# One slot 480 bytes longer: where weight tiles and activation slots begin in a partition

## The chip, the core and the metric

The program runs on one core of a Trainium2 chip. What counts is the device time of one execution in microseconds (us). In the profile PE is TensorE's matmul side, PEld its weight loads, DVE VectorE, ACT ScalarE, POOL GpSimd and SP the engine that issues the transfers.

## What is computed

Two transformer blocks, one after the other, on 512 tokens of width 1024, all in float32. Cut to its products, the reference is:

```python
def first_block(x, mem, ...):
    proj = rmsnorm(x) @ w_in                    # 1024 -> 1536: pool mixer, gating unit
    h = x + concat([pool_mixer(p), sgu_mixer(u, v)]) @ w_out
    h = h + mem_cross_attention(rmsnorm(h), mem, wq, wk, wv, wo)   # 4 heads, 256 memory rows
    h = h + conv_ffn(rmsnorm(h), w_up, conv_w, conv_b, w_down)     # 1024 -> 2*2816 -> 1024
    return rmsnorm(h)

def second_block(x, ...):
    q, k, v, glu_a, glu_b = split(rms_norm(x) @ w_in)
    attn = stick_breaking_attention(rms_norm(q), rms_norm(k), v)   # 8 heads
    c = silu(layer_norm(causal_depthwise_conv(glu_a * sigmoid(glu_b))))   # 31 taps
    x = x + concat([attn, c]) @ w_out
    gate, val = split(rms_norm(x) @ w_up)
    return x + (silu(causal_depthwise_conv(gate)) * val) @ w_down
```

## The kernel before

**Products.** Each float32 operand is held as two tiles, a rounded high part (h) and the rest (l), and each product is three matmuls (`mm3`, lines 122 to 125): high by high, high by low, low by high. The first operand of `pe.matmul` after the output is the stationary one, loaded 128x128 ahead of the matmul; the second streams past it (the moving one, mostly 512 columns). Every matmul of `mm3` has a stationary block of its own to load.

**Weights.** A unit is 128x2048 floats. `prep` (lines 174 to 205) transfers it into `raw`, ScalarE casts it into `whi` (line 195) and VectorE subtracts for `wlo` (line 196); `weights` keeps two units ready. `raw`, `whi` and `wlo` have two buffers each. In `sta_unit` (line 212) 128x128 blocks of `whi` and `wlo` are stationary and the activations move: 48 matmuls for a unit with 8 steps of k, in the order whi, whi, wlo. In `mov_stage` (line 222), `project` and `values` the weights move and activations are stationary. Three early units of the second block (`split_early`, line 676) are not in `whi` and `wlo` but in the slots F, G and E.

**Slots.** Activations live in slots of 128x2048 floats, named A0 to H1 (`slot`, line 145); a name is used again and again, as a tile of its own each time. H0 and H1 are longer: `slot("H0", F32R, 2176)` and `slot("H1", F32R, 2056)` at line 403, the same sizes again at lines 637, 905 and 992.

**Where tiles begin.** Each partition is filled in the order constants, slots in the order in which their names first occur, weight tiles, temporary tiles. In the built program the slots come as A0, A1, B0, B1, C0, C1, D0, G0, E0, E1, F0, F1, G1, H0, H1, D1. A slot is 8192 bytes in a partition (16 times 512), H0 8704 (17 times 512), H1 8224 (16 times 512 and 32). A0 begins 96 bytes beyond a multiple of 512 and so do all slots up to H1; D1, which lies behind H1, and then raw, whi, wlo and t2 begin 128 beyond one. A step of k, of a unit's block or of 128 tokens is a multiple of 512 bytes, so that every block of a tile begins at its tile's remainder. The trace names a tile by its letter alone: D stands for D0 and D1.

**The order around the change.** The program order on each engine is set by a scheduler when the kernel is built. In the first block's feed-forward (`evac1`, lines 648 to 657), each unit's result goes from PSUM into H (line 651, after a small memset at line 650), through three taps (lines 643 to 646), a Silu (line 656) and a product (line 657); `work` (line 639) hands out the two halves of H0 and H1 in turn. `col(16)` (line 113) gives small tiles with 8 buffers: four are asked for in the pool mixer (line 390), four in the two calls of `heads` (line 730).

Of the kernel before, what the change touches and what calls it, by code (L numbers as in the profile page):

```python
# [10 lines left out]
F32 = mybir.dt.float32  # L11
F32R = mybir.dt.float32r
# [4 lines left out]
P = 128  # L17
# [3 lines left out]
KC = D // P  # L21
M = 256
# [53 lines left out]
def block_kernel(  # L76
# [17 lines left out]
    tp = ctx.enter_context(tc.tile_pool(name="tp", bufs=4))  # L94
# [16 lines left out]
        return tp.tile([P, 512], F32, tag="t2", name="t2", bufs=2)  # L111

    def col(n):
        return tp.tile([P, n], F32, tag=f"col{n}", name=f"col{n}", bufs=8)

    def keep(name, n=4):
        return const.tile([P, n], F32, tag=name, name=name)
# [27 lines left out]
    def slot(name, dt=F32R, cols=2048):  # L145
        return slots.tile([P, cols], dt, tag=name, name=name)

    def part(tl, a, b, at=0):
        return tl[:, at : at + a * b].rearrange("p (a b) -> p a b", a=a)
# [161 lines left out]
    def mean_col(tiles, w, n=D):  # L311
        nt = w // P
        ps = single()
        chunks = [tl[:, j, :] for tl in tiles for j in range(tl.shape[1])]
        for t in range(nt):
            for i, ch in enumerate(chunks):
                pe.matmul(ps[:, t : t + 1], ch[:, t * P : (t + 1) * P], ones[:, 0:1],  # L317
                          start=i == 0, stop=i == len(chunks) - 1)
        m = col(4)
        dve.tensor_scalar(m[:, :nt], ps[:, :nt], 1.0 / n, EPS, ALU.mult, ALU.add)  # L320
        return m

    def rsqrt(m, n, name=None):
        o = keep(name) if name else col(4)
        pool.tensor_tensor(o[:, :n], m[:, :n], mhalf[:, :n], ALU.pow)
        return o
# [37 lines left out]
    for u in range(2):  # L364
# [23 lines left out]
        for j in range(2):  # L388
            g = 2 * u + j
            hd = col(16)  # L390
            dve.tensor_tensor(hd, sums[j][:, 0:16], par("inv", 16 * g, 16), ALU.mult)
            dve.scalar_tensor_tensor(sums[j], sums[j], 0.5 ** (g + 1), p[:, j, :],
                                     ALU.mult, ALU.subtract)
            dve.tensor_tensor(sums[j][:, 0:16], hd, p[:, j, 0:16], ALU.subtract)
            copy_split(dh[:, g, :], dl[:, g, :], sums[j])
# [4 lines left out]
    gr = slot("G1")  # L400
    sgh, sgl, plh, pll = (part(gr, 4, P, 512 * i) for i in range(4))
    memst = Stats(M)
    mh, ml = part(slot("H0", F32R, 2176), KC, M), part(slot("H1", F32R, 2056), KC, M)

    pool.affine_select(out=sgw, in_=sgw, compare_op=ALU.is_ge, fill=0.0, base=0,
                       pattern=[[0, 4], [1, P]], channel_multiplier=-1)
# [227 lines left out]
        down(2)  # L634

    turn = [0]
    ht = [slot("H0", F32, 2176), slot("H1", F32, 2056)]

    def work(n):
        turn[0] = (turn[0] + 1) % 4  # L640
# [462 lines left out]
```

## Time and profile before

| | us |
|---|---|
| median of three runs | 1275.32 |
| lowest, highest | 1274.69, 1275.57 |
| the profiled execution | 1275.78 |
| its span, first to last instruction | 1274.1 |
| TensorE's granted clock, mean | 0.996 of full speed |
| PE busy | 1257.1 (99%) |
| PEld busy | 1011.6 (79%) |
| DVE busy | 772.2 (61%) |
| ACT busy | 485.1 (38%) |

Matmuls overlap in the pipeline: a 128x512 matmul is shown as about 396 ns long, but the next one starts well before it ends. What a matmul costs in a stream is the distance from its start to the next one's start, called the pitch below. It is read from the timeline, whose start times have two decimals, over many matmuls.

### The profile page before, as it was taken

How to read it: one execution, taken by the hardware profiler on the slowest of the kernel's cores; microseconds unless marked ns; L12 is line 12 of the kernel's file. 1: busy time of each engine (PE TensorE's matmuls, PEld its weight loads, DVE VectorE, ACT ScalarE, POOL GpSimd, SP SyncE). 2: the span in 40 equal slices, each digit the busy share in tenths (PEclk: the TensorE clock that was granted, in tenths of full speed). 3: DMA queues.
4: the chain of work that ended last, by engine and by line, in shares of the span. 5: the costliest groups of instructions: out<-in, count | busy, mean ns of one | idle time of the engine just before them, and what ended most of it. 6: DMA issues, size and time to landing. Idle time of an engine off the chain costs nothing.

```text
span 1274.1 us, 13633 instructions
## 1 busy us (share of the span) xinstructions
PE 1257.1 (99%) x5712; PEld 1011.6 (79%) x5712; DVE 772.2 (61%) x813; ACT 485.1 (38%) x528; POOL 108.7 (9%) x125
## 2 busy tenths in 40 slices
PE   9999999999999999999999899999999999999998
PEld 6888888788888888888887678667888888888887
DVE  7845624744866664466366999976675555336522
ACT  6432524532544432243253225873443333213310
POOL 1100210012000000000054411000400000000000
PEclk9999999999999999999999989999999999999999
DMA  7233222312222222222343001101222222222212
GB/s 285 91 112 109 99 99 74 126 66 100 94 77 95 99 99 99 100 82 85 116 149 132 0 34 67 67 1 66 99 100 99 76 90 99 100 100 100 87 63 81
DMA packets 20445, 118.32 MB, mean 93 GB/s; under 512 B 2208, under 2 KB 4128, under 8 KB 7712
## 3 DMA queue, kind: packets, MB, share of 16 engines
q1 hardware_dynamic: 20096, 117.20, 26.1%
q8 instruction: 44, 0.72, 0.2%
q10 hardware_dynamic: 288, 0.26, 0.1%
q14 instruction: 17, 0.14, 0.0%
HBM read 115.35 MB, written 2.10 MB: 92 GB/s over the span
## 4 chain that ended last, share of the span: by engine, by line
PE 92%; DVE 4%; ACT 2%; issue 1%; POOL 1%; DMA 0%; SPq 0%; DVEq 0%; ACTq 0%
PE pp L124 28%; PE pp L125 28%; PE pp L123 28%; DVE H L832 2%; PE ps L123 1%; PE ps L124 1%; PE ps L125 1%; POOL col L739 0%; DVE H L698 0%; PE ps L317 0%; PE ps L813 0%; DVE t L785 0%; PE pp L774 0%; DMA A<-in_xT 0%; ACT t L783 0%
## 5 line engine op out<-in xcount | busy, mean ns | idle before, releaser
L195 ACT CAST whi<-raw 128x2048 fp32r<-128x2048 f32 (+3 forms) x109 | 197.8, 1815 | 452.4 <-PE pp L124 381.9
L196 DVE TENSOR_TENSOR wlo<-raw,whi 128x2048 fp32r<-128x2048 f32 (+3 forms) x109 | 236.8, 2173 | 73.2 <-ACT whi L195 72.6
L123 PE MATMUL pp<-B,whi 128*128 128x512 f32 x672 | 265.8, 397 | 1.0 <-ACT whi L195 1.0
L125 PE MATMUL pp<-B,wlo 128*128 128x512 f32 x672 | 266.3, 396 | 0.2
L124 PE MATMUL pp<-C,whi 128*128 128x512 f32 x672 | 266.0, 396 | 0.0
L124 PE MATMUL pp<-G,whi 128*128 128x512 f32 x448 | 177.8, 397 | 0.0
L125 PE MATMUL pp<-F,wlo 128*128 128x512 f32 x416 | 164.9, 396 | 0.0
L123 PE MATMUL pp<-F,whi 128*128 128x512 f32 x416 | 164.2, 396 | 0.0
L123 PEld LDWEIGHTS pp<-B,whi 128*128 128x128 f32 x672 | 126.3, 188 | 32.1 <-ACT whi L195 1.8
L125 PEld LDWEIGHTS pp<-B,wlo 128*128 128x128 f32 x672 | 126.2, 188 | 32.1 <-DVE wlo L196 1.5
L124 PEld LDWEIGHTS pp<-C,whi 128*128 128x128 f32 x672 | 126.3, 188 | 30.7 <-issue 0.5
L124 PEld LDWEIGHTS pp<-G,whi 128*128 128x128 f32 x448 | 84.2, 188 | 20.4 <-issue 0.2
L625 DVE TENSOR_TENSOR A<-pp,A 128x1024 f32<-128x1024 f32 x23 | 28.2, 1225 | 112.2 <-PE pp L125 112.2
L125 PEld LDWEIGHTS pp<-F,wlo 128*128 128x128 f32 x416 | 78.2, 188 | 19.0 <-issue 0.2
L646 DVE SCALAR_TENSOR_TENSOR H<-H,sm,H 128x512 f32<-128x512 f32 x132 | 92.8, 747 | 0.7
L123 PEld LDWEIGHTS pp<-F,whi 128*128 128x128 f32 x416 | 78.1, 188 | 19.0 <-issue 0.2
L832 DVE SCALAR_TENSOR_TENSOR H<-H,sm,H 128x512 f32<-128x512 f32 x120 | 88.3, 765 | 1.2
L651 DVE TENSOR_TENSOR H<-pp,rb 128x1024 f32<-128x1024 f32 x22 | 26.9, 1224 | 56.2 <-PE pp L125 49.8
L128 ACT ACTIVATE H<-H,sm 128x512 f32<-128x512 f32 x70 | 54.2, 808 | 9.8 <-DVE H L698 9.8
L997 DVE TENSOR_TENSOR H<-pp,rb 128x512 f32<-128x512 f32 x22 | 15.2, 692 | 67.7 <-PE pp L125 61.3
L124 PE MATMUL pp<-E,whi 128*128 128x512 f32 x112 | 44.3, 396 | 0.0
L123 PE MATMUL pp<-D,whi 128*128 128x512 f32 x112 | 44.2, 395 | 0.0
(293 smaller groups left out, 1808.8 us busy)
## 6 DMA issues: line engine op xcount, KB each, us to landing
raw<-in_wts SPq DMA_DIRECT2D x99, 1024.0 KB, 4.8
raw<-in_wts SPq DMA_DIRECT2D x8, 768.0 KB, 4.2
A<-in_xT SPq DMA_DIRECT2D x3, 512.0 KB, 6.8
out<-A SPq DMA_DIRECT2D x3, 512.0 KB, 2.8
D<-in_memT SPq DMA_DIRECT2D x1, 1024.0 KB, 11.6
raw<-in_wts SPq DMA_DIRECT2D x3, 256.0 KB, 7.1
A<-in_xT SPq DMA_DIRECT2D x2, 256.0 KB, 3.4
raw<-in_wts SPq DMA_DIRECT2D x2, 128.0 KB, 3.6
```

Source lines behind the costliest of these rows:

```text
L123: pe.matmul(out, wh, xh, start=start, stop=False, **kw)
L124: pe.matmul(out, wh, xl, start=False, stop=False, **kw)
L125: pe.matmul(out, wl, xh, start=False, stop=stop, **kw)
L128: act.activation(out, in_, AF.Identity, scale=scale, bias=bias)
L195: act.copy(hi[:, cs], raw[:, cs])
L196: dve.tensor_tensor(lo[:, cs], raw[:, cs], hi[:, cs].bitcast(F32), ALU.subtract)
L625: dve.tensor_tensor(hu, pt, hu, ALU.add)
L646: dve.scalar_tensor_tensor(dst, hs[:, k : k + 512], w(k), dst, ALU.mult, ALU.add)
L651: dve.tensor_tensor(hs[:, :, 2:], pt, over2(rb), ALU.mult)
L832: tap = dve.scalar_tensor_tensor(cv[:, i, :], cc[:, i, k : k + 512], par("dw_w", 4 * k + i), cv[:, i, :], ALU.mult, ALU.add)
L997: dve.tensor_tensor(hs[:, 2:514], pt[:, 0, :], rb, ALU.mult)
```

## The change

H1 gets 2176 columns as H0 has, which is 480 bytes more in each partition (8704 bytes, 17 times 512). All that lies behind it moves by 480: D1, raw, whi, wlo and t2 now begin 96 bytes beyond a multiple of 512, as the slots before H1 do. The three buffers of t4, 128, 256 and 384 before, begin at 96, 224 and 352, the two of acc at 480 instead of 0. The 16-wide small tile has 6 buffers instead of 8, 128 bytes less.

```diff
     def col(n):
-        return tp.tile([P, n], F32, tag=f"col{n}", name=f"col{n}", bufs=8)
+        return tp.tile([P, n], F32, tag=f"col{n}", name=f"col{n}", bufs=6 if n == 16 else 8)
...
-    mh, ml = part(slot("H0", F32R, 2176), KC, M), part(slot("H1", F32R, 2056), KC, M)
+    mh, ml = part(slot("H0", F32R, 2176), KC, M), part(slot("H1", F32R, 2176), KC, M)
...
-    ht = [slot("H0", F32, 2176), slot("H1", F32, 2056)]
+    ht = [slot("H0", F32, 2176), slot("H1", F32, 2176)]
```

No engine gets an instruction more or less, and none changes its place. What differs is a few waits around H1 in `evac1`. On GpSimd, in the first block's feed-forward (H_2137 is H0, H_2138 is H1; lines with a minus are of the kernel before):

```order
 L650 MEMSET H_2137 128x2x2 [waits DVE_49,Activation_49]
-L650 MEMSET H_2138 128x2x2 [waits DVE_49]
+L650 MEMSET H_2138 128x2x2 [waits DVE_49,Activation_49]
 L650 MEMSET H_2137 128x2x2 [waits DVE_49,Activation_49]
-L650 MEMSET H_2138 128x2x2 [waits DVE_49,Pool_49]
+L650 MEMSET H_2138 128x2x2 [waits DVE_49,Activation_49]
```

The memset of H1 waits for ScalarE as well, as that of H0 does; on VectorE the instruction of line 651 that writes H1 then waits for GpSimd, which before stood at the first tap behind it (line 646).

## Rows read from the trace of the kernel before

**Rows 1.** The page: busy time by engine (with its share of the span and the number of instructions), then the chain that ended last, by engine and by line.
```profile
PE 1257.1 (99%) x5712; PEld 1011.6 (79%) x5712; DVE 772.2 (61%) x813; ACT 485.1 (38%) x528; POOL 108.7 (9%) x125
PE 92%; DVE 4%; ACT 2%; issue 1%; POOL 1%; DMA 0%; SPq 0%; DVEq 0%; ACTq 0%
```

**Rows 2.** Busy time in a stretch of 100 us. Columns: the stretch, its length, then busy us with the number of instructions for PE, PEld, DVE, ACT and POOL, the granted clock, DMA's share and GB/s.
```profile
400.00:500.00 100.00, 100.00 (x430) 80.54 (x430) 63.37 (x66) 37.84 (x42) 0.82 (x8) 1.00 0.27 95
```

**Rows 3.** Timeline of PE in the first block's feed-forward, 520 to 534 us: start, shown length, line, output<-moving,stationary tile. The rows shown are the first two and the last of 62 matmuls that follow on each other.
```profile
519.66 0.40 PE L124 MATMUL pp<-E,whi 128*128 128x512 f32 x1
519.89 0.39 PE L125 MATMUL pp<-D,wlo 128*128 128x512 f32 x1
...
533.88 0.40 PE L125 MATMUL pp<-F,wlo 128*128 128x512 f32 x1
```

**Rows 4.** Timeline of PE in the second block, 690 to 694 us and 699.8 to 713.3 us: the end of a weight unit from whi and wlo, then `mov_stage` with the early units of slots F and G moving and slots B and C stationary. Between the rows of 691.24 and 693.30 8 matmuls are left out; from 699.83 to 713.20 there are 60 matmuls with these two ends.
```profile
690.77 0.40 PE L124 MATMUL pp<-C,whi 128*128 128x512 f32 x1
691.01 0.40 PE L125 MATMUL pp<-B,wlo 128*128 128x512 f32 x1
691.24 0.39 PE L123 MATMUL pp<-F,B 128*128 128x512 f32 x1
...
693.30 0.39 PE L123 MATMUL pp<-F,B 128*128 128x512 f32 x1
...
699.83 0.39 PE L123 MATMUL pp<-G,B 128*128 128x512 f32 x1
...
713.20 0.39 PE L125 MATMUL pp<-G,C 128*128 128x512 f32 x1
```

**Rows 5.** Timeline of PE in the first block's `mov_stage`, 34 to 38 us, where whi and wlo move and slots B and C are stationary: the first row and the last of 18 matmuls that follow on each other.
```profile
33.61 0.40 PE L125 MATMUL pp<-whi,C 128*128 128x512 f32 x1
...
37.58 0.40 PE L124 MATMUL pp<-wlo,B 128*128 128x512 f32 x1
```

**Rows 6.** Weight loads on PEld by tiles, first in 520 to 534 us, then in 698 to 713 us: busy us, mean ns of one, idle time before them.
```profile
L123 PEld LDWEIGHTS pp<-F,whi 128*128 128x128 f32 x19 | 3.6, 188 | 0.9
L123 PEld LDWEIGHTS pp<-G,B 128*128 128x128 f32 x14 | 2.6, 188 | 0.5
```

**Rows 7.** Timeline of PE in the pool mixer's product (slots E moving, G1 stationary), 78.6 to 82 us: the second and the last of its 12 matmuls and the one behind them.
```profile
79.06 0.39 PE L124 MATMUL pp<-E,G 128*128 128x512 f32 x1
...
81.37 0.40 PE L125 MATMUL pp<-E,G 128*128 128x512 f32 x1
81.61 0.28 PE L123 MATMUL pp<-H,whi 128*128 128x256 f32 x1
```

**Rows 8.** Timeline of PE in the cross-attention's product of probabilities and values, 246.8 to 252 us: slots F and G move, D0 (lines 123 and 124) and D1 (line 125) are stationary. From 246.88 to 251.08 there are 18 matmuls.
```profile
246.88 0.40 PE L123 MATMUL pp<-F,D 128*128 128x512 f32 x1
247.11 0.40 PE L124 MATMUL pp<-G,D 128*128 128x512 f32 x1
247.35 0.39 PE L125 MATMUL pp<-F,D 128*128 128x512 f32 x1
...
251.08 0.39 PE L123 MATMUL pp<-B,whi 128*128 128x512 f32 x1
```

**Rows 9.** Timeline of PE where 256 columns move: slots E against B and C in the scores, 36 matmuls from 200.59 to 204.90, then H against whi and wlo, 10 matmuls from 94.75 to 95.93.
```profile
200.59 0.28 PE L123 MATMUL pp<-E,B 128*128 128x256 f32 x1
...
204.90 0.40 PE L123 MATMUL ps<-whi,H 128*128 128x512 f32 x1
...
94.75 0.28 PE L123 MATMUL pp<-H,whi 128*128 128x256 f32 x1
...
95.93 0.28 PE L124 MATMUL pp<-H,whi 128*128 128x256 f32 x1
```

**Rows 10.** Instructions that read or write whi, then those of wlo, by stretches: length, busy us with count for PE, PEld, DVE and (whi) ACT, clock, DMA.
```profile
0.00:690.00 690.00, 576.97 (x1885) 349.52 (x1886) 142.72 (x67) 119.27 (x67) 1.00 0.31 109
690.00:870.00 180.00, 67.79 (x212) 39.30 (x212) 14.64 (x7) 13.36 (x7) 0.97 0.10 36
870.00:1274.00 404.00, 357.93 (x1137) 213.26 (x1136) 79.46 (x36) 65.12 (x35) 1.00 0.26 91
0.00:690.00 690.00, 366.20 (x942) 176.99 (x942) 142.72 (x67) 1.00 0.31 109
690.00:870.00 180.00, 42.20 (x107) 19.90 (x106) 14.64 (x7) 0.97 0.10 36
870.00:1274.00 404.00, 224.92 (x569) 106.72 (x568) 79.46 (x36) 1.00 0.26 91
```

**Rows 11.** Busy time by stretches in the middle of the second block, columns as in rows 2.
```profile
690.00:735.00 45.00, 39.76 (x171) 31.71 (x169) 39.87 (x42) 12.22 (x12) 18.91 (x12) 0.93 0.07 25
735.00:760.00 25.00, 25.00 (x102) 20.21 (x101) 22.69 (x30) 4.06 (x5) 0.00 (x0) 0.92 0.12 43
800.00:840.00 40.00, 36.02 (x247) 25.24 (x246) 39.11 (x48) 36.80 (x46) 0.00 (x0) 1.00 0.14 52
```

**Rows 12.** Timeline of POOL, ACT and DVE around a unit of the first feed-forward, 338 to 354 us: the memset, the Silu and the reading of PSUM into H.
```profile
338.89 0.10 POOL L650 MEMSET H<- 128x4 f32 x1 [9.20 <-DVE H L646]
338.14 0.63 ACT L656 ACTIVATE H<-H 128x512 f32<-128x512 f32 x1 [3.06 <-DVE H L646]
342.62 1.23 DVE L651 TENSOR_TENSOR H<-pp,rb 128x1024 f32<-128x1024 f32 x1 [1.67 <-PE pp L125]
```

## The prediction

> **What bounds the kernel now.** I read the page's first part and the chain of waits first. PE is busy for 1257.1 of 1274.1 us, and the chain that ended last is 92% PE and 4% DVE [rows 1]. So nearly everything is one stream of matmuls, and the question is what one matmul costs in it. A stretch of 100 us in the feed-forward holds 430 matmuls with PE never idle and the clock at its full share [rows 2]. The timeline gives the pitch more closely: from 519.66 to 533.88 us there are 61 steps, 14.22 / 61 = 0.2331 us [rows 3]. At the granted full clock of 2.4 GHz 512 columns would be 512 / 2.4 = 213.3 ns, so about 20 ns of each matmul are something else, in a stream without waits. Whether the change can take some of that away is the whole case, because it adds and removes no instruction.
>
> The trace holds the experiment already. At 691.24 us PE goes over from a unit of whi and wlo to `mov_stage` with early units in slots. There both the moving tiles (F, G) and the stationary ones (B, C) are slots that begin 96 bytes beyond a multiple of 512, while nearly everywhere else one of the two is whi or wlo, at 128. The shape, the three matmuls of a product and a new stationary block for each are the same. From 699.83 to 713.20 us there are 59 steps: 13.37 / 59 = 0.2266 us [rows 4]. That is 6.5 ns less than 233.1, through 60 matmuls in a row. The same function in the first block, with whi and wlo moving at 128 and slots B and C stationary at 96, has 17 steps in 3.97 us, 0.2335 [rows 5]: one function, one order of the three products, and what differs for PE is where its tiles begin. The engines beside PE do not explain it: VectorE is busy for 39.87 of 45 us around that stretch [rows 11], and 63.37 of 100 in the feed-forward [rows 2]; PE is faster beside the busier one.
>
> The lower pitch is not there at once. From 691.24 to 693.30, at the entry, 9 steps take 2.06 us, 0.229 each [rows 4]. The pool mixer's 12 matmuls, where E and G1 are both at 96, are over before they are past such an entry: 11 steps from 79.06 to 81.61 us, 0.232 [rows 7]. I take that as one thing: a stream in which all tiles have one remainder settles to 226.6 after some eight matmuls, and an odd tile keeps it from settling. Where D1, at 128, is the stationary tile of one matmul in three, 18 matmuls take 4.20 us, 0.2333, though the other two have equal remainders [rows 8]. So equality in most matmuls buys nothing; all have to be equal, and this is what the move of D1 and of all weight tiles by 480 bytes gives.
>
> **The change part by part.**
>
> *Matmuls with 512 columns and a tile of whi or wlo.* Up to 690 us 1885 and 942 matmuls touch whi and wlo [rows 10], of which 192 move only 256 columns (k of the cross-attention: 4 units of 16 blocks, three matmuls each): 1885 + 942 - 192 = 2635. From 870 us on it is 1137 + 569 = 1706, of which 32 have acc as the moving tile (half of the convolution's part of the output projection), which goes from 0 to 480 and stays odd: 1674. Together 4309. All the other tiles of these streams (B to G, H0, and now D1 and t2) will begin at 96. If each settles, the gain is 4309 x (233.1 - 226.6) = 4309 x 6.5 ns = 28.0 us, all of it on the path, since PE never idles in these stretches.
>
> *The middle, 690 to 870 us.* 212 + 107 = 319 such matmuls lie here [rows 10]. They would give at most 2.1 us, but VectorE is busy for 39.87 of 45 us, 22.69 of 25 and 39.11 of 40 [rows 11]; it carries the 31-tap convolution, and PE waits for it. I take 0.5 us, with 0 and 2.1 as ends.
>
> *The product with D1.* 48 matmuls at 233.3 ns [rows 8] would settle too: 48 x 6.7 = 0.3 us gained.
>
> *Matmuls with 256 columns.* Equal remainders are worse here: in the scores 36 steps take 4.31 us, 0.1197, while H against whi and wlo takes 1.18 us for 10, 0.118 [rows 9]. 192 matmuls go from the second kind to the first: 192 x 1.7 ns = 0.3 us lost.
>
> *Entries.* Each time the stream is broken by another tile or a wait (the sums of the norms against constant tiles, the transposes, the values between the scores), it has to settle again. An entry costs 9 matmuls at 229 instead of 226.6, 0.02 us [rows 4]; an odd tile in between may cost as much as 8 x 6.5 ns = 0.05. With some 30 such places I take 1.0 us; the ends are 0.5 and 3.
>
> *Waits around H1.* The memset of H1 on GpSimd now waits for ScalarE, and the reading of PSUM into H1 on VectorE waits for the memset. Behind it on VectorE stand the split of the next weights and the taps; PE would wait for them last. The tile H0 has these waits already, and the trace shows what they cost: the Silu ends at 338.14 + 0.63 = 338.77, the memset runs at 338.89 for 0.10 us, and the next reading of PSUM begins at 342.62, for PE's sake [rows 12]. The unit that comes next is 48 x 6.5 ns = 0.3 us earlier after the change, against a slack of 3.6 us. So this is nothing; without that cover it would be 0.1 us in each of 11 units, 1.1 us in all.
>
> *Fewer small tiles.* With 6 buffers instead of 8 the last requests in `heads` take buffers that the pool mixer used and left hundreds of us before. Nothing.
>
> *ScalarE, VectorE and the transfers.* raw, whi and wlo have one remainder before and after, so no row prices their moves; I leave casts and subtractions as they are. Should they get 0.1 us longer or shorter they would still be hidden: a unit has 48 x 0.2266 = 10.9 us, and VectorE is busy for 63% of the time in the feed-forward stretch shown [rows 2].
>
> The sum: 28.0 + 0.5 + 0.3 - 0.3 - 1.0 = 27.5 us gained. The profiled execution took 1275.78 us, its span 1274.1, with 1.7 us around it that do not change. 1275.78 - 27.5 = 1248.3; the median of the three runs is 0.5 below the profiled one, so 1275.32 - 27.5 = 1247.8. I say 1248.
>
> **A rule against the change.** The weight loads are shown with 188 ns in the slow stream and in the quick one [rows 6]. So the load's own time does not tell the two apart, and the pitch does. The Trainium skill, "TensorE: Matmul & The Clock Gate", Part 2, Step-by-step, says that PE has two independent SBUF read ports, so that loading the next stationary block takes no bandwidth from the running matmul. By that rule where the two tiles begin would change nothing, and the time would stay at 1275.3. The trace does not agree in so far as the pitch depends on the pair of tiles: 233.1 [rows 3] and 226.6 [rows 4].
>
> **The rivals.**
>
> 1. *The quick stretch is quick for another reason, and nothing changes* (1275.3). For it: in it the weights move, while in most of the kernel they are stationary, and no stretch of the trace has weights at rest in a stream of equal remainders. Against it: the weights move in the first block's `mov_stage` too, and there the pitch is 0.2335 [rows 5]. 6%.
>
> 2. *The stream settles only in part.* If other work breaks it up again and again, it stays in the entry's mean of 0.229 to 0.232 [rows 4, 7]: 4309 x (233.1 - 231.8) = 5.6 us up to 4309 x (233.1 - 229) = 17.7 us gained, 1258 to 1270. For it: the pool mixer never settled. Against it: 60 matmuls in a row did without one odd step, with VectorE at work all the time. 10%.
>
> 3. *Slower: the loss of the 256-column streams is what equal remainders do, and it comes to the 512-column ones with the weights at rest.* There a settled stream of equal remainders has 1.7 ns more for each matmul [rows 9]. Paid in 4309 matmuls it is 7.3 us, 1282.6. It decides from the first 200 matmuls of the first units on. For it: it is a settled stream, of 36 matmuls, and its stationary tiles change every second or third matmul as in `sta_unit`. Against it: with 512 columns the only settled stream went the other way, by four times as much. 4%.
>
> **How the numbers follow.** The forecast, settling nearly everywhere, has 80%: 1248, with its own ends at 1275.3 - (28.0 + 2.1 + 0.3 - 0.5) + 0.3 = 1245.7 and, with entries at 3 us, the waits at 1.1 and nothing from the middle, 1275.3 - (28.0 + 0.3 - 0.3 - 3 - 1.1) = 1251.4. A pitch read from two decimals is good to 0.2 ns, 1 us either way. So 1244.5 to 1252.5 for the forecast alone; a stream that is unsettled for a fifth of its matmuls would add 5.6 us to 1248, and to hold the time in 8 of 10 cases I let the range reach over most of that: 1244 to 1256. What a measurement of this kernel can tell from no change is about 0.2%, 2.6 us. Faster by more than that are the forecast and rival 2, 80 + 10 = 90%; within it is rival 1 with 6%; slower is rival 3 with 4%.
>
> **What would show it right or wrong.** In the profile of the changed kernel a stretch of 100 us in the feed-forward should hold 441 matmuls instead of 430, and the timeline there should have a pitch of 0.2266 with a shown length near 0.39 instead of 0.40. The scores should stay at 0.12, k of the cross-attention go from 0.118 to 0.12, the product with D1 from 0.2333 to 0.2266. VectorE's chain between 690 and 735 us should take as long as before. A pitch that stays at 0.233 where all tiles begin at 96 would make the prediction wrong at its root; one that goes to and fro between 0.225 and 0.236 means rival 2; and a PE that begins to wait for wlo or H in the feed-forward would show a cover that I counted on gone.

## The result, and the profile after

| | before | after |
|---|---|---|
| median, us | 1275.44 | 1246.88 |
| lowest, highest, us | 1274.69, 1276.63 | 1246.36, 1247.21 |
| the profiled execution, us | 1275.78 | 1246.8 |
| its span, us | 1274.1 | 1245.1 |

The kernel after takes 0.9775 of the time before, with a 95% interval of 0.9758 to 0.9792, from four runs of each. It is faster by 28.56 us between the medians, 29.0 between the profiled executions; the forecast had 27.5.

The page of the kernel after, busy time by engine and the chain that ended last by engine:

```profile
PE 1226.2 (98%) x5712; PEld 1009.9 (81%) x5712; DVE 771.2 (62%) x813; ACT 485.2 (39%) x528; POOL 110.0 (9%) x125
...
PE 92%; DVE 4%; ACT 2%; issue 1%; POOL 1%; DMA 0%; SPq 0%; DVEq 0%; ACTq 0%
```

Against [rows 1] one number has moved: PE has 30.9 us less, with the same 5712 matmuls. The other engines work as long as before, and the chain has the same shares: no new wait has taken the place of the gain, the same stream has become shorter.

Busy time in a stretch of the kernel after, columns as in [rows 2]:

```profile
400.00:500.00 100.00, 100.00 (x443) 82.81 (x442) 60.06 (x61) 36.09 (x38) 0.71 (x7) 1.00 0.27 95
```

443 matmuls where 430 stood, at the same granted clock of 1.00, again without an idle moment. The timeline of PE in the kernel after, first block's feed-forward, names the pitch; the three rows are the first two and the last of 63 matmuls that follow on each other:

```profile
519.82 0.39 PE L124 MATMUL pp<-G,whi 128*128 128x512 f32 x1
520.05 0.39 PE L125 MATMUL pp<-F,wlo 128*128 128x512 f32 x1
...
533.87 0.39 PE L123 MATMUL pp<-F,whi 128*128 128x512 f32 x1
```

62 steps in 14.05 us are 0.2266 us, where [rows 3] gave 0.2331. The cross-attention's product with D0 and D1, in the kernel after:

```profile
243.03 0.39 PE L123 MATMUL pp<-F,D 128*128 128x512 f32 x1
...
247.79 0.39 PE L123 MATMUL pp<-B,whi 128*128 128x512 f32 x1
```

21 steps in 4.76 us are 0.2267, against 0.2333 in [rows 8]. And k of the cross-attention, 256 columns, in the kernel after:

```profile
86.98 0.28 PE L124 MATMUL pp<-H,whi 128*128 128x256 f32 x1
...
88.78 0.28 PE L124 MATMUL pp<-H,whi 128*128 128x256 f32 x1
```

15 steps in 1.80 us are 0.120, against 0.118 in [rows 9]: the one kind of stream that became slower, as foretold.

**Where the 29.0 us came from.** The 5712 matmuls stand in the same order with the same operands in both traces, so each step from one start to the next can be set beside its counterpart. Up to the first matmul of the early units (691.24 us before, [rows 4]; 675.79 after) 15.45 us are gained, from there to line 895 (863.61 before, 845.46 after) 2.70, and from there to the end 10.82. By kind of step, worked out from all steps of the two profiled executions, where a 512-column step between 200 and 250 ns counts as one without a wait:

| us gained | forecast | measured |
|---|---|---|
| 512-column steps without a wait, up to the early units | 17.1 + 0.3, less entries | 16.99 |
| the same, from the early units to line 895 | 0.5 | 1.70 |
| the same, from line 895 on | 10.9, less entries | 10.87 |
| entries, all stretches | -1.0 | in the rows above |
| 256 columns | -0.3 | -0.33 |
| waits and other matmuls, up to the early units | 0 | -1.22 |
| the same, in the middle | 0 | 1.01 |
| the same, at the end | 0 | -0.05 |
| sum | 27.5 | 28.97 |

Two lines, -1.22 and 1.01, nobody had foretold. The first comes from one wait at the start. PE in the kernel before, then in the kernel after, at the seventh matmul of the first unit:

```profile
8.25 0.50 PE L123 MATMUL pp<-B,whi 128*128 128x512 f32 x1 [0.16 <-ACT whi L195]
```
```profile
9.33 0.50 PE L123 MATMUL pp<-B,whi 128*128 128x512 f32 x1 [1.71 <-ACT whi L195]
```

It waits 0.16 us for the first weights in one execution, 1.71 in the other. The step that ends there took between 0.24 and 2.09 us in the eleven timed kernels of this study, without order: 2.09 in the kernel after, 0.44 in e10_small, which has the same pitch, 1.20 in e7_cols6, which has the old one. So this wait is not the change's. The second is the clock. Windows of the kernel before, then of the kernel after, at the same place of the program, where PE goes over from the transposes to the third early unit:

```profile
735.00:739.00 4.00, 4.00 (x11) 3.17 (x10) 4.00 (x4) 1.63 (x2) 0.00 (x0) 0.50 0.12 16
```
```profile
719.30:723.30 4.00, 4.00 (x16) 3.21 (x15) 4.00 (x4) 1.63 (x2) 0.00 (x0) 0.76 0.17 25
```

The last but two column is the granted clock: 0.50, the lower level of 1.2 GHz, against 0.76, which is both levels in one stretch. In both PE had waited ahead of it for the transposed values from VectorE (line 741), 1.71 us the last time before, 2.08 after. Five matmuls of 0.43 us in the trace before are one of 0.26 and four of some 0.23 after. Over the eleven timed kernels one to five of these are long in the five with the old pitch, none to three in the six where most streams or all have the new one. The two overlap, so how much of the 1.01 us belongs to the change is not shown.

### The profile page after: what moved, and what is told of

Same layout as the page of the kernel before. It is cut to its first block, busy times and chain, and to the rows that moved or that the text cites. A ratio compares the mean times of both kernels' runs of the same rounds, so it can differ in the third digit from the quotient of the medians.

```text
span 1245.1 us, 13634 instructions
## 1 busy us (share of the span) xinstructions
PE 1226.2 (98%) x5712; PEld 1009.9 (81%) x5712; DVE 771.2 (62%) x813; ACT 485.2 (39%) x528; POOL 110.0 (9%) x125
## 4 chain that ended last, share of the span: by engine, by line
PE 92%; DVE 4%; ACT 2%; issue 1%; POOL 1%; DMA 0%; SPq 0%; DVEq 0%; ACTq 0%
PE pp L125 28%; PE pp L123 28%; PE pp L124 28%; DVE H L832 2%; PE ps L123 1%; PE ps L124 1%; PE ps L125 1%; POOL col L739 0%; PE ps L317 0%; DMA A<-in_xT 0%; PE ps L813 0%; DVE t L785 0%; PE pp L774 0%; ACT t L783 0%; PE pp L745 0%
## 5 line engine op out<-in xcount | busy, mean ns | idle before, releaser
L123 PE MATMUL pp<-B,whi 128*128 128x512 f32 x672 | 261.7, 390 | 2.4 <-ACT whi L195 2.4
L125 PE MATMUL pp<-B,wlo 128*128 128x512 f32 x672 | 262.1, 390 | 0.2
L124 PE MATMUL pp<-C,whi 128*128 128x512 f32 x672 | 261.8, 390 | 0.0
L124 PE MATMUL pp<-G,whi 128*128 128x512 f32 x448 | 175.1, 391 | 0.0
L125 PE MATMUL pp<-F,wlo 128*128 128x512 f32 x416 | 162.2, 390 | 0.0
L123 PE MATMUL pp<-F,whi 128*128 128x512 f32 x416 | 161.5, 389 | 0.0
L651 DVE TENSOR_TENSOR H<-pp,rb 128x1024 f32<-128x1024 f32 x22 | 26.8, 1224 | 50.6 <-PE pp L125 44.4
```

Of the source, the lines that this page charges most:

```text
L123: pe.matmul(out, wh, xh, start=start, stop=False, **kw)
L124: pe.matmul(out, wh, xl, start=False, stop=False, **kw)
L125: pe.matmul(out, wl, xh, start=False, stop=stop, **kw)
L651: dve.tensor_tensor(hs[:, :, 2:], pt, over2(rb), ALU.mult)
```

## The experiments

The forecast's theory, A: all tiles of a stream, moving and stationary, have to begin at one remainder by 512; where they are does not matter, and one odd tile spoils the stream. Its rivals: P, that each matmul counts by the pair of its own two tiles; that the remainder itself (96) or merely a distance is what helps; that a finer remainder than 512 is enough; and that the gain comes from another part of the edit. Unless a text says otherwise, the experiments are edits of the kernel after, timed beside the kernel before.

### Which distances are good

The length of H1 sets the distance between the slots (96) and all that lies behind them. In four kernels it is the one thing changed (the lines are cut to the slot; lines 403 and 637 change alike):

```diff
-slot("H1", F32R, 2176)
+slot("H1", F32R, 2064)     e1_off64:  weights at 160, 64 bytes from the slots' 96
+slot("H1", F32R, 2080)     e2_off128: at 224, 128 bytes
+slot("H1", F32R, 2104)     e8_off224: at 320, 224 bytes
+slot("H1", F32R, 2112)     e3_off256: at 352, 256 bytes
```

> H1 has 2064 columns, so that D1 and the weight tiles begin 64 bytes beyond the slots' remainder (160 against 96), not 0 as in the changed kernel and not 32 as in the kernel before. Theory A (the stream settles only when all its tiles begin at the same place by 512 bytes): pitch 0.233 in the feed-forward, 1275 us. Theory B (a smaller grain is enough, 64 bytes): pitch 0.2266, 1247 us. Theory C (not equality counts, only where the weights themselves begin): some third pitch, not to be told from the trace so far.

> H1 has 2080 columns: D1 and the weight tiles begin 128 bytes beyond the slots' remainder (224 against 96). Theory A (512): 0.233, 1275 us. Theory B (64) and a grain of 128: 0.2266, 1247 us. Where the run with 64 bytes is slow and this one quick, the grain is 128.

> H1 has 2104 columns: D1 and the weight tiles begin 224 bytes beyond the slots' remainder (320 against 96), which is 32 bytes short of 256, where the kernel before had 32 bytes too much. Theory A with a grain of 256: not settled, 1270 to 1275 us. If the stream settles over a window of offsets on one side of 256 (the weights a little ahead): 0.2266 or less, 1247 us.

> H1 has 2112 columns: D1 and the weight tiles begin 256 bytes beyond the slots' remainder (352 against 96). Theory A (512): 0.233, 1275 us. A grain of 64, 128 or 256: 0.2266, 1247 us. Where the runs with 64 and 128 bytes are slow and this one quick, the grain is 256.

| weights less slots, bytes | median, us | ratio to before | matmuls from 400 to 500 us |
|---|---|---|---|
| 32 (before) | 1275.44 | 1 | 430 |
| 64 | 1273.19 | 0.9982 (0.9972 to 0.9991) | 431 |
| 128 | 1271.96 | 0.9972 (0.9961 to 0.9982) | 432 |
| 224 | 1275.58 | 0.9998 (0.9988 to 1.0007) | 431 |
| 256 | 1246.67 | 0.9774 (0.976 to 0.9789) | 443 |
| 0 (after) | 1246.88 | 0.9775 (0.9758 to 0.9792) | 443 |

The stretch from 400 to 500 us of e8_off224, then of e3_off256:

```profile
400.00:500.00 100.00, 100.00 (x431) 80.44 (x430) 63.69 (x66) 37.85 (x41) 0.82 (x8) 1.00 0.27 95
```
```profile
400.00:500.00 100.00, 100.00 (x443) 82.83 (x442) 60.27 (x61) 36.52 (x38) 0.72 (x7) 1.00 0.27 95
```

A distance of 256 bytes is as good as none, and 32 bytes less than that is worth nothing. So the remainder that has to agree is the one by 256, and a remainder by 512 asks for more than is needed. The 64 and 128 bytes have a small gain of 2 to 3.5 us, and their intervals leave out 1; their streams do not settle (the series further down show where the gain may come from).

### Whether the place itself matters

In e4_all0 three constants change their pool, so that every slot and every weight tile begins at a multiple of 512:

```diff
-        return const.tile([P, n], F32, tag=name, name=name)
+        return (tp if name in ("rr", "rr2", "r3") else const).tile([P, n], F32, tag=name, name=name, bufs=1)
```

> Three small constants of 32 bytes are moved from before the slots to behind the weight tiles, so that all slots and all weight tiles begin at a multiple of 512 instead of 96 beyond one; all differences between them stay. If only equality counts: as the changed kernel, 1246.9 us, pitch 0.2266. If the place itself counts too (96 is 32 beyond a multiple of 64, 0 is not): another pitch, lower if a start inside a line of 64 bytes is what is left of the 13 ns over 512 columns at the full clock; at 215 ns for each of some 4600 matmuls it would be 1246.9 - 4600 x 11.6 ns = 1194 us at the most.

1246.38 us, ratio 0.9775 (0.9758 to 0.9791), 443 matmuls in the stretch: the same as with all at 96. Of the two places tried neither is better: agreement counts, not the place.

### Whose agreement: the matmul's own pair, or the stream's

e5_b_odd makes slot B1 32 bytes longer, so that A and B begin at 96 and all slots and weights behind them at 128; the 16-wide small tile has one buffer less:

```diff
-        return tp.tile([P, n], F32, tag=f"col{n}", name=f"col{n}", bufs=6 if n == 16 else 8)
+        return tp.tile([P, n], F32, tag=f"col{n}", name=f"col{n}", bufs=5 if n == 16 else 8)
...
-        return slots.tile([P, cols], dt, tag=name, name=name)
+        return slots.tile([P, 2056 if name == "B1" else cols], dt, tag=name, name=name)
```

> B1 gets 8 columns more, so that A and B begin at 96 and all the other slots (C to H, D1) and all weight tiles at 128. The streams without B (F with G, D with E, H) have equal remainders, at 128; in those with B, 2016 matmuls with weights at rest, 240 with weights moving and 144 of the early units, two tiles of three or one of three are 32 bytes off. Theory A (all tiles of a stream have to agree, by 256 bytes): the streams without B at 0.2266, those with B at 0.233 in all three matmuls, 1246.9 + 2400 x 6.5 ns = 1262.5 us. Theory P (each matmul pays for its own pair of moving and stationary tile alone): only the 1600 matmuls that read B pay, 1246.9 + 10.4 = 1257.3 us, and C against whi stays at 0.2266.

1260.71 us, ratio 0.9882 (0.9867 to 0.9897). In a unit with B and C two of three matmuls have an odd pair (B at 96, weights at 128), while C with whi is an equal one, 128 and 128. Timeline of PE in e5_b_odd, such a unit; its first row and its last are 42 steps apart:

```profile
284.10 0.40 PE L123 MATMUL pp<-B,whi 128*128 128x512 f32 x1
284.33 0.39 PE L124 MATMUL pp<-C,whi 128*128 128x512 f32 x1
284.56 0.40 PE L125 MATMUL pp<-B,wlo 128*128 128x512 f32 x1
284.80 0.40 PE L123 MATMUL pp<-B,whi 128*128 128x512 f32 x1
...
293.90 0.40 PE L123 MATMUL pp<-B,whi 128*128 128x512 f32 x1
```

9.80 / 42 = 0.2333. Over all such units the mean steps from the three matmuls are 234.2, 230.7 and 234.0 ns: the one with the equal pair is some 3 ns better off than its neighbours and 4 above 226.7. Units with D and E, or F and G, all at 128, have 226.7. P would want C at 226.7 too, and 693 ns for the three steps together, 2 x 233.3 + 226.7; they take 699, as three in the kernel before. Of the totals A's was 1.8 us too high and P's 3.4 too low; where A's 1.8 went was not followed up, and the single units decide.

e6_d1_odd makes D1 alone odd: H1 is back at its old length, and D1 is as much longer as brings the weights back to 96 (the first pair of lines is cut to the slot):

```diff
-slot("H1", F32R, 2176)
+slot("H1", F32R, 2056)
...
-        return slots.tile([P, cols], dt, tag=name, name=name)
+        return slots.tile([P, 2168 if name == "D1" else cols], dt, tag=name, name=name)
```

> H1 has 2056 columns as before and D1 120 more, so that D1 begins at 128 as in the kernel before, and the weight tiles at 96 as in the changed one; the waits around H1 are those of the kernel before. Theory A: the 288 matmuls of the streams with D1 (with E1, with G1 and in the product with the values) go back to 0.232 to 0.233, the rest stays at 0.2266, 1246.9 + 288 x 6.5 ns = 1248.8 us. Theory P: only the 144 that read D1 pay, 1247.8 us; the two are told apart by the pitch in the streams with G1. If the waits around H1 had cost something, up to 1.1 us come off.

1249.21 us, ratio 0.9792 (0.9778 to 0.9807), 2.33 us above the kernel after, though the two intervals overlap; what decides is the pitch. Timeline of PE in e6_d1_odd, a unit that works on D1 and E1 first, then on D0 and E0, then on the first two again (D stands for both):

```profile
484.78 0.40 PE L123 MATMUL pp<-D,whi 128*128 128x512 f32 x1
...
489.68 0.39 PE L123 MATMUL pp<-D,whi 128*128 128x512 f32 x1
489.90 0.39 PE L124 MATMUL pp<-E,whi 128*128 128x512 f32 x1
...
495.12 0.40 PE L123 MATMUL pp<-D,whi 128*128 128x512 f32 x1
```

From 484.78 to 489.68, with D1, 21 steps take 4.90 us, 0.2333. From 489.68 to 495.12, with D0, 24 steps take 5.44, 0.2267. Same engine, same unit, same shape, no wait on either side: the odd tile alone makes the step, and E1 with whi, an equal pair, is slow among the odd ones (232 ns on average).

The streams with G1, by which the expectation wanted to tell A from P, have an equal pair in two matmuls of three; only D1 is odd. Timeline of PE in e6_d1_odd, the first three and the last of 25 matmuls that follow on each other (here G stands for G1, D for D1, and the last row is of the next stream):

```profile
1171.86 0.39 PE L123 MATMUL pp<-G,whi 128*128 128x512 f32 x1
1172.08 0.40 PE L124 MATMUL pp<-D,whi 128*128 128x512 f32 x1
1172.32 0.39 PE L125 MATMUL pp<-G,wlo 128*128 128x512 f32 x1
...
1177.42 0.39 PE L123 MATMUL pp<-G,whi 128*128 128x512 f32 x1
```

24 steps take 5.56 us, 0.2317; P would have (2 x 226.7 + 233.3) / 3 = 228.9 ns. That is A again and not P.

### The other parts of the edit

e7_cols6 is the kernel before with the shorter row of small tiles alone, e10_small the kernel before with H1 at 2112 columns and nothing else, the small tiles as they were:

```diff
e7_cols6:
-        return tp.tile([P, n], F32, tag=f"col{n}", name=f"col{n}", bufs=8)
+        return tp.tile([P, n], F32, tag=f"col{n}", name=f"col{n}", bufs=6 if n == 16 else 8)
e10_small (cut to the slot; lines 403 and 637 change alike):
-slot("H1", F32R, 2056)
+slot("H1", F32R, 2112)
```

> The kernel before with 6 buffers for the 16-wide small tile instead of 8, and nothing else: no tile that TensorE reads moves. Theories A and P: 1275.4 us as before. If the smaller count cost a wait in the heads of the second block: some tenths of a us more.

> The kernel before with 2112 columns for H1, so that D1 and the weight tiles begin 256 bytes beyond the slots' remainder, and all 8 buffers of the 16-wide small tile kept: the shortest form of the change if the grain is 256. Theory A with a grain of 256: 1246.7 us as in the run with 256 bytes. If the smaller number of buffers had paid for something: slower or quicker by some tenths.

e7_cols6: 1276.16 us, ratio 1.0002 (0.9992 to 1.0011). e10_small: 1246.61 us, ratio 0.9768 (0.9755 to 0.9781). The small tiles cost and bring nothing that can be measured, and e10_small is the shortest form of this change, with 256 bytes less for H1 than in the kernel after. It is as quick as the kernel after, whose interval overlaps; no version of the study is quicker beyond the measurement.

### The pair by itself

e9_series is the kernel after with series of 48 matmuls behind its end, in which the moving tile (E0) and the stationary one (F0), both at 96, are shifted against each other. It ran once. `mt` is E0 and `st_` is F0; `o` counts floats of 4 bytes, so that 8 is a shift of 32 bytes. Each series sums into one PSUM bank and waits for nothing:

```diff
+    def series(o, n=512, m=128, count=48, step=128):
+        ps = single(0)
+        for i in range(count):
+            at, c = step * (i % 12), 512 * ((i // 3) % 3) + o
+            yield dict(out=ps[:m, :n], lhsT=st_[:, at : at + m], rhs=mt[:, c : c + n], start=i == 0,
+                       stop=i == count - 1)
...
+    for a in series(0): pe.matmul(**a)
...
```

> The changed kernel with series of matmuls behind its last product, whose results nobody reads, to measure the pitch by itself; nothing of the computation is left out. Slot E0 (96 bytes beyond a multiple of 512) moves, slot F0 (96 too) is stationary, in 48 matmuls a series; from series to series the moving window starts 0, 4, 8, 16, 32, 48, 64, 96, 128, 160, 192, 224, 256, 384 and 512 bytes further on. Theory A with a grain of 256 bytes: 0.2266 at 0, 256 and 512, about 0.23 to 0.234 at all the others, at 384 too; below 32 bytes the kernel has no row, the settled pitch may reach over a few bytes. If the meeting of the weight load and the stream is what costs: with 32 stationary columns instead of 128 (a quarter of the load) the offset of 32 bytes costs less than 6.6 ns, at the least 1.6; if the streams of moving tiles alone make the pitch, it still costs 6.6. With one stationary block for all 48 matmuls nothing changes, as each still loads it.

Timeline of PE in e9_series, one row for each series of 48: its start, what it took, its line. Lines 1033, 1034, 1037, 1041, 1045, 1046 and 1047 have the moving tile 0, 4, 32, 128, 256, 384 and 512 bytes on:

```profile
1265.15 11.21 PE L1033 MATMUL ps<-E,F 128*128 128x512 f32 x48
1276.42 11.66 PE L1034 MATMUL ps<-E,F 128*128 128x512 f32 x48
...
1311.10 11.46 PE L1037 MATMUL ps<-E,F 128*128 128x512 f32 x48
...
1356.98 11.41 PE L1041 MATMUL ps<-E,F 128*128 128x512 f32 x48
...
1403.07 11.21 PE L1045 MATMUL ps<-E,F 128*128 128x512 f32 x48
1414.33 11.46 PE L1046 MATMUL ps<-E,F 128*128 128x512 f32 x48
1425.85 11.16 PE L1047 MATMUL ps<-E,F 128*128 128x512 f32 x48
```

Equal tiles, and tiles apart by 256 or 512 bytes, take 11.2 us; the others, those left out here too, 11.3 to 11.7. The entry of each series is in these times; the mean of the last 35 steps, from their starts in the trace, leaves it out:

| moving less stationary, bytes | 0 | 4 | 16 | 32 | 64 | 128 | 192 | 256 | 384 | 512 |
|---|---|---|---|---|---|---|---|---|---|---|
| ns, 512 columns | 226.7 | 237.5 | 231.6 | 233.3 | 229.0 | 232.4 | 233.3 | 226.7 | 233.5 | 226.7 |
| ns, 256 columns | 120.0 | | | 116.7 | | 118.7 | | 120.0 | | |

So the effect needs nothing of this kernel but the two tiles, and it has no slope: the multiples of 256 are good, nothing else is. It is there when the stationary block is the same one each time (226.7 at 0, 233.3 at 32). With 32 stationary columns instead of 128, a smaller load (shown with 109 ns instead of 188), the stream does not settle at any of the three offsets tried: 231.6 at 0, 233.2 at 32, 230.7 at 128. So the choice that the expectation wanted from these columns is not decided.

How much a bad distance costs depends on its direction: 64 bytes on cost less (229.0) than 192 (233.3), which by 256 is 64 bytes back. e1_off64 has both, since its weights begin 64 bytes beyond the slots: with weights at rest its tiles are at 192 by this table, with weights moving at 64. Its mean 512-column steps without a wait are 233.2 ns with weights at rest and 230.1 with weights moving, where the kernel before has 233.2 and 233.4. e2_off128, at 128 either way, has 232.3 with weights at rest, near the 232.4 of the table.

e11_series2 has more series of this kind, among them shorter streams, fewer stationary columns and tiles that change their offset from matmul to matmul; here the shifts of the moving and the stationary tile in floats are functions of the matmul's number `i`, the first and `s`:

```diff
...
+    for a in series(m=64): pe.matmul(**a)
+    for a in series(n=480): pe.matmul(**a)
+    for a in series(lambda i: 32 * (i % 2)): pe.matmul(**a)
+    for a in series(s=lambda i: 32 * (i % 2)): pe.matmul(**a)
+    for a in series(lambda i: 8 * i % 64, s=lambda i: 8 * i % 64): pe.matmul(**a)
...
```

> The changed kernel with a second set of series behind its last product, whose results nobody reads; nothing of the computation is left out. All tiles begin at 96, 48 matmuls a series. From the first set: settled, 256 columns take 120.0 ns and 512 take 226.7, which is 13.3 ns over the columns at the full clock both times. Theory A with a fixed 13.3 ns: 384 columns 173.3, 448 columns 200.0, and 480, 496 and 508 columns, which end off a grain of 256 bytes though they begin on one, still 213.3, 220.0 and 225.0; if the length of the stream counts, by a sixteenth of it, 384 take 170 and 448 take 198. Windows that alternate by 256 bytes: 226.7; by 32, 64 or 128 bytes, moving or stationary: not settled, 229 to 234. Moving and stationary windows that go on together by 32 or 64 bytes from matmul to matmul: 226.7 if only the difference within a pair counts, 229 to 234 if neighbours have to agree too. Another PSUM bank for every matmul or always the same moving window: 226.7. Any series below 226 would be a way to a kernel quicker than the changed one.

| series | ns |
|---|---|
| moving tile 0 and 128 bytes on in turns; 0 and 256 | 230.0; 226.7 |
| stationary tile 0 and 128 bytes on in turns; 0 and 256 | 232.3; 226.7 |
| both move on together by 32 bytes a matmul, by 64 | 232.6; 228.3 |
| stationary columns 64, 96, 112 | 230.0, 230.0, 228.8 |
| moving columns 384, 448, 480, 496, 508 | 173.3, 202.7, 216.5, 220.0, 227.6 |

Timeline of PE in e11_series2, one row for each series of 48: the moving tile 0 and 256 bytes on in turns, then both tiles on together by 32 bytes a matmul, then by 64:

```profile
1391.21 11.18 PE L1044 MATMUL ps<-E,F 128*128 128x512 f32 x48
...
1493.80 11.43 PE L1053 MATMUL ps<-E,F 128*128 128x512 f32 x48
1505.30 11.24 PE L1054 MATMUL ps<-E,F 128*128 128x512 f32 x48
```

The third row of the table is the sharpest: there each matmul has an equal pair, and the pitch is still 232.6. A tile has to agree with the tiles of the matmuls beside it, too. The offsets of 252 and 508 bytes give the same 229.7, and 64 and 320 bytes 229.0 and 228.8: the pattern repeats every 256. The expectation for other lengths was missed: 384, 496 and 512 columns have 13.3 ns more than columns / 2.4, but 448, 480 and 508 have 15.9 to 16.5, so that 508 columns are slower than 512. No series went below 226.7 for 512 columns.

## Why the prediction was right, and where it was off

**What the root of it said held.** The pitch of a 512-column matmul in these streams is set by where its tiles begin. The steps without a wait went from a mean of 233.23 ns to 226.90 up to the early units, and from 233.23 to 226.91 at the end, with weights at rest as with weights moving. Rival 1 (another reason for the quick stretch) is out by e6_d1_odd, where a single tile makes and unmakes it inside one unit; rival 3 (the loss of the 256-column streams also with 512) by 443 matmuls in 100 us; rival 2 (settling in part) by the mean, which is 0.2 to 0.3 ns above the settled 226.7.

**One odd tile in three matmuls spoils the stream.** This was inferred from 18 matmuls [rows 8]. e6_d1_odd bears it out where D1 is one tile of three (231.7 ns), and e5_b_odd has one equal pair of three that does not settle either. The series that move on together widen it: neighbours have to agree.

**By 512 was too much.** The step "all tiles of a stream must have one remainder by 512" cost the forecast nothing, since the change makes all of them equal by 512 anyway, but it is too strong: 256 bytes do (e3_off256, e10_small). In the trace of before tiles 256 bytes apart meet in 512-column matmuls only one or two at a time (the products with a constant at line 801), too few to settle, so it could not tell.

**Terms that were mis-sized.** The middle stretch, 0.5 us, gave 1.70. The forecast took VectorE's high share there for a bound, but in most of it PE's is higher. Windows of the kernel before, then after, in the second part of this stretch:

```profile
733.33:863.61 130.28, 125.98 (x673) 95.31 (x674) 116.08 (x142) 74.93 (x87) 9.86 (x8) 0.98 0.12 41
```
```profile
717.62:845.46 127.84, 123.58 (x672) 94.51 (x673) 115.96 (x142) 74.91 (x87) 9.86 (x8) 0.99 0.12 42
```

PE is busy for 125.98 of 130.28 us, VectorE for 116.08; 2.44 us go here, of which the clock has about 1.0. From the early units to this point, 42.09 us before and 41.83 after, 0.26 go, little, as the forecast thought of the whole stretch. The ends of the term, 0 and 2.1, held. Entries were taken at 1.0 us. What the steps after the change have above the settled 226.66 ns is (226.90 - 226.66) x 2681 + (227.31 - 226.66) x 411 + (226.91 - 226.66) x 1721 = 1.3, near it; the steps before were 0.13 ns longer on average than the 233.1 of the sum, which gave 0.6 us back. The wait at the start and the clock in the middle, -1.22 and 1.01, nearly cancel, which helped the total and was no merit of the forecast.

**The waits around H1** cost nothing that can be seen. The instruction of line 651 got the new wait, for the memset of [rows 12]. The page's groups of the kernel before, then of the kernel after (busy us, mean ns of one, idle time of VectorE ahead of it and what ended most of that):

```profile
L651 DVE TENSOR_TENSOR H<-pp,rb 128x1024 f32<-128x1024 f32 x22 | 26.9, 1224 | 56.2 <-PE pp L125 49.8
```
```profile
L651 DVE TENSOR_TENSOR H<-pp,rb 128x1024 f32<-128x1024 f32 x22 | 26.8, 1224 | 50.6 <-PE pp L125 44.4
```

VectorE is idle there for 56.2 us before and 50.6 after, for PE's sake but for 6.4 and 6.2 us; GpSimd has not come in between.

**The rule.** The pitch depends on how the stationary tiles lie to the moving ones, 226.7 against 233.3 ns in e9_series, with nothing else different. The Trainium skill, "TensorE: Matmul & The Clock Gate", Part 2, Step-by-step, has the next block's load take no read bandwidth from the running matmul; by that rule, as the prediction read it, the time would have stayed at 1275.3. The measured 1246.88 decides against that reading for these tiles; whether it is the reading of the buffer that meets, no run shows.

**What stays open.** That the load of a block and the stream of another meet somewhere inside is a reading that suits the runs, but none shows where, nor which neighbour a tile has to agree with: with equal pairs that move on by 64 bytes the pitch is 228.3, by 32 bytes 232.6. Why a load of fewer columns does not settle, why 256-column streams are 3 ns quicker when they do not agree, and what the 13.3 ns are that a settled matmul still takes beyond its columns, no run here tells.

## What to carry to other kernels

Where a stream of 512-column matmuls sets the time, each with a load of its own, look at the start addresses of its tiles: all tiles, moving and stationary, of all matmuls that follow on each other, at one remainder by 256 bytes, and one odd buffer in a pool (a padded tile, an odd constant) undoes it for every stream that touches it or what lies behind it. Streams of 256 columns went the other way here, so the length of the stream has to be asked first. A stretch of the same shape that runs at another pitch in the same trace is a free experiment; ask first what differs in its operands. Where an engine looks like the bound by its busy share, set the other engines' shares of the same stretch beside it before a gain is written off.

## What the hardware showed that was not expected

- The remainder that counts is by 256 bytes, and near misses are worth nothing: 224 bytes of distance gave 1275.58 us, 256 gave 1246.67.
- A distance of 4 bytes is the worst of all, 237.5 ns, slower than every larger one tried.
- With 256 columns agreement costs: 120.0 ns against 116.7.
- A stationary block of 32, 64 or 96 columns makes the stream no quicker than 128 do, 231.6, 230.0 and 230.0 against 226.7.
- 508 moving columns take 227.6 ns, 512 take 226.7.
